# The decoded samples' attention products with queries and probabilities loaded in four 32-column groups and the cache moving

## The chip, the cores and the metric

The kernel runs on one core of a Trainium2 chip. The metric is the device time of one execution in microseconds (us). The time before is the median of three runs, 2102.01 us (2100.24, 2102.01 and 4988.29). One further execution was profiled; every row below is from it.

## The reference

The program is one layer of a hybrid decoder: a prompt of 1024 tokens and eight sequences ("samples") that each decode one token against a carried cache. The change touches only the attention of the samples. Cut to that part:

```python
# samples: kc, vc are the cached 127 keys and values and the new one: (8, 128, 4 kv heads, 64)
kc = concat([cache_k, new_k])[-128:]
vc = concat([cache_v, new_v])[-128:]
s = einsum('qhgd,khd->hgqk', qg, kc) * 64 ** -0.5      # 16 query heads, 4 to a kv head
p = softmax(concat([s, sink]))[..., :-1]
o_b = einsum('hgqk,khd->qhgd', p, vc)                  # then @ w_swa_out
```

So there are 8 samples x 16 heads = 128 score rows of 128 keys, and 128 output rows of 64 channels. Around it stand the projections of all 1032 tokens, the prompt's sliding-window attention, a gated delta rule in chunks with eight heads, an output mix, and a feed-forward part, all in float32.

## The kernel before

The prompt's projections run as three TensorE products of split operands (`mm3`, lines 180 to 182). The prompt's attention is done in four groups of two query tiles (`attention_group`), each group in eight blocks of 128 queries (`attention_block`, called n = 0 to 7). In a block, TensorE makes scores (lines 615 and 616), ScalarE and VectorE mask them into `E` and make a softmax (lines 619 to 638), TensorE transposes `E` into `pt` (line 190), VectorE masks it into `pc` and `pp` (lines 643 and 647), and TensorE multiplies with `V` into `pv` (line 653), which ScalarE copies out (line 655).

The samples' attention is put in at the start of the last group (g = 3). It has three steps. `sample_cache` has loaded keys and values, 128 window positions by 256 channels for each sample, into four tiles named `qst`, and has put the samples' queries into `qa`, a tile whose rows are the 128 channels of two kv heads and which is zero where a head does not use a channel. `sample_keys` transposes the keys in place. `sample_softmax` then makes scores, a softmax over `ps` and `pr` with small sums in `sk`, and the values' product.

Before the change, both products load the cache as the stationary operand, one 128x128 block for each sample and each pair of kv heads, and move eight columns (the queries or probabilities of that sample) past it: sixteen products at line 709 and sixteen at line 736. The scores come out with the keys as rows, so they are copied to `st` (line 710) and transposed. The softmax gives `pr` with one row for each sample and head; `pr` is transposed and copied to `pT` (line 732) for the values. Their product has channels as rows, and sixteen small copies (line 740) put it into `obs`, which goes to memory.

Each engine takes its instructions in one fixed order. A scheduler makes that order when the program is built, from priorities and its own costs; `later(f, by)` gives a step a lower priority. The fillers of group 3 are projections taken in pieces:

```python
if g == 3:
    for _ in range(2 if n < 6 else 18):
        with self.tc.issue_after(self.scored.ins):
            self.later(lambda: next(self.filler), 120)
```

After the attention come the eight delta-rule heads, in which a recursion over eight chunks (lines 946 to 962) alternates TensorE with ScalarE and VectorE while projections fill in between.

Of the kernel before, what the change touches and what calls it, by code (L numbers as in the profile page):

```python
# [18 lines left out]
P = 128  # L19
NP = 1024  # L20
NS = 8
# [43 lines left out]
class Step:  # L65
# [591 lines left out]
    def sample_cache(self, pool, psum, kx, vx):  # L657
        nc, I = self.nc, self.I

        tp = self.t(self.pmf, [NS, 4, P], "mm")  # L660
        for i in range(2):
            self.transpose(tp[:, i, :], kx[:, i, P:136])
            self.transpose(tp[:, 2 + i, :], vx[:, i, :])
        new = self.t(pool, [NS, 512], "new", bufs=1)
        nc.vector.tensor_copy(new, tp.rearrange("b i c -> b (i c)"))
        newd = self.t(self.dr, [1, 2, NS, 256], "newd")
        for c in range(2):
            nc.sync.dma_start(newd[0, c], new[:, c * 256:(c + 1) * 256])

        kv = []  # L670
        for c, (cache, out) in enumerate(((I["cache_swa_k"], self.O[7]), (I["cache_swa_v"], self.O[9]))):
            halves = []
            for b in (0, 4):
                kc = self.t(pool, [P, 4, 256], "qst")
                nc.sync.dma_start(kc, cache[0][b:b + 4].rearrange("b w g d -> w b (g d)"))
                nc.sync.dma_start(kc[0:1], newd[:, c, b:b + 4])
                halves.append(kc)
            kv.append(halves)
            old = lambda a, w: a[0][:, w:w + 127].rearrange("b w g d -> b (w g d)").rearrange("b (s e) -> s b e", s=16)
            with self.tc.issue_after(self.w_load.ins):  # L680
                nc.sync.dma_start(old(out, 0), old(cache, 1))
            nc.sync.dma_start(out[0][:, 127].rearrange("b g d -> b (g d)"), newd[0, c])

        qa = self.t(pool, [P, 2, NS, 8], "qa", bufs=1)
        nc.gpsimd.memset(qa, 0.0)
        for hq in range(16):
            p, r, g = hq // 8, hq % 8, hq // 4
            src = self.qs[(hq % 2) * 64:(hq % 2) * 64 + 64, hq // 2, :]
            nc.vector.tensor_copy(qa[(g % 2) * 64:(g % 2) * 64 + 64, p, :, r], src)
        self.samples = kv, qa  # L690

    def sample_keys(self):
        kc = self.samples[0][0]
        for half in kc:
            for p in range(2):
# [2 lines left out]
                    self.transpose(tp[:, b, :], half[:, b, p * P:(p + 1) * P])  # L698
                self.nc.scalar.copy(half[:, :, p * P:(p + 1) * P], tp)

    def sample_softmax(self, pool, psum):
        nc, I = self.nc, self.I
        (kc, vc), qa = self.samples

        scores = self.t(pool, [P, 2, NS, 8], "st", bufs=1)
        sc = self.t(self.pmf, [P, 2, NS, 8], "mm")
        for b in range(NS):
            for p in range(2):
                nc.tensor.matmul(sc[:, p, b, :], kc[b // 4][:, b % 4, p * P:(p + 1) * P], qa[:, p, b, :], start=True, stop=True)
        nc.vector.tensor_copy(scores, sc)  # L710
        ps = self.t(self.pmf, [P, P], "mm")
        self.transpose(ps, scores.rearrange("k p b r -> k (p b r)"))

        sk = self.t(pool, [P, 8], "sk", bufs=1)
        sinkc = self.t(pool, [P, 1], "sinkc", bufs=1)
        for p in range(2):
            src = I["swa_sinks"][0][p * 8:p * 8 + 8].rearrange("(r o) -> r o", o=1)
            nc.sync.dma_start(sinkc[p * 64:p * 64 + 64, :], src.unsqueeze(0).broadcast_to([NS, 8, 1]))
        nc.vector.tensor_reduce(sk[:, 0:1], ps, axis=AX.X, op=ALU.max)
        nc.vector.tensor_tensor(sk[:, 0:1], sk[:, 0:1], sinkc, op=ALU.max)  # L720
        nc.vector.tensor_tensor(sk[:, 1:2], sinkc, sk[:, 0:1], op=ALU.subtract)
        nc.scalar.activation(sk[:, 2:3], sk[:, 1:2], AF.Exp)
        nc.vector.tensor_scalar_mul(sk[:, 3:4], sk[:, 0:1], -1.0)
        pr = self.t(pool, [P, P], "pr", bufs=1)
        nc.scalar.activation(pr, ps, AF.Exp, bias=sk[:, 3:4], accum_out=sk[:, 4:5])
        nc.vector.tensor_tensor(sk[:, 5:6], sk[:, 4:5], sk[:, 2:3], op=ALU.add)
        nc.vector.reciprocal(sk[:, 6:7], sk[:, 5:6])
        nc.vector.tensor_scalar_mul(pr, pr, sk[:, 6:7])
        ps = self.t(self.pmf, [P, P], "mm")
        self.transpose(ps, pr)  # L730
        pT = self.t(pool, [P, 2, NS, 8], "pT", bufs=1)
        nc.vector.tensor_copy(pT.rearrange("k p b r -> k (p b r)"), ps)
        pv = self.t(self.pmf, [P, 2, NS, 8], "mm")
        for p in range(2):
            for b in range(NS):
                nc.tensor.matmul(pv[:, p, b, :], vc[b // 4][:, b % 4, p * P:(p + 1) * P], pT[:, p, b, :], start=True, stop=True)
        obs = self.t(pool, [P, 8, NS], "obs", bufs=1)
        for hq in range(16):
            p, r, g = hq // 8, hq % 8, hq // 4
            nc.vector.tensor_copy(obs[(hq % 2) * 64:(hq % 2) * 64 + 64, hq // 2, :],  # L740
                                  pv[(g % 2) * 64:(g % 2) * 64 + 64, p, :, r])
        nc.sync.dma_start(self.ob[:, :, NP:NT].rearrange("i p b -> p i b"), obs)
# [1314 lines left out]
```

## Time and profile before

| | value |
|---|---|
| time of the profiled execution | 2099.13 us |
| its span | 2097.4 us |
| granted TensorE clock, mean | 0.983 |
| TensorE (PE) busy | 2027.4 us, 97% |
| weight loads (PEld) busy | 1924.1 us, 92% |
| VectorE (DVE) busy | 1362.2 us, 65% |
| ScalarE (ACT) busy | 902.8 us, 43% |
| share of the chain that ended last: PE / DMA / DVE | 77% / 8% / 6% |

Rows of time read: start in us, duration in us, engine, line, operation, output and inputs, shape, count. A float32 product appears as two records, one for each of its passes, so sixteen products are "x32"; a transpose and a product of split operands have one. Rows by window give, for each engine, busy us and the number of instructions, then the granted TensorE clock (1.00 is full), the share of DMA time and GB/s. PE busy time is modelled and counts an instruction until its result has landed, so it also covers some latency.

### The profile page before, as it was taken

The numbers are of one execution on the slowest core, as the hardware profiler recorded it, in microseconds if no ns is written. First come the engines' busy times: TensorE is split into PE (matmuls) and PEld (weight loads), VectorE is DVE, ScalarE is ACT, GpSimd is POOL, SyncE is SP. The second block draws the span as 40 slices with busy tenths as digits, with TensorE's granted clock in tenths as the row PEclk, the third lists the DMA queues.
The fourth block names the chain that finished last, engine by engine and source line by source line (L and its number), as shares of the span: only waits on it lengthen the run. The fifth ranks groups of instructions, "written<-read, shape, count | busy, mean of one in ns | idle before, by whom it ended". The sixth has DMA issues, their size and how long they took to land.

```text
span 2097.4 us, 41330 instructions
## 1 busy us (share of the span) xinstructions
PE 2027.4 (97%) x16245; PEld 1924.1 (92%) x16245; DVE 1362.2 (65%) x2733; ACT 902.8 (43%) x2233; POOL 520.2 (25%) x594
## 2 busy tenths in 40 slices
PE   7999999999999999989999999999999999999998
PEld 3987778799999999989988999999999999999898
DVE  4756667564736647566554575479876776778875
ACT  3665545433333342442442452245544544544543
POOL 1000000021321211201211000004556556445530
PEclk8999999899999999999999999999999999999999
DMA  7246344152232312312266774413333333487972
GB/s 270 88 140 213 127 148 140 39 147 62 74 83 55 81 58 70 84 36 70 63 193 188 251 230 134 139 58 93 99 97 112 96 97 92 137 295 272 310 233 84
DMA packets 301887, 275.75 MB, mean 131 GB/s; under 512 B 59730, under 2 KB 248111, under 8 KB 301676
## 3 DMA queue, kind: packets, MB, share of 16 engines
q1 hardware_dynamic: 295852, 252.22, 39.2%
q0 software_dynamic: 5552, 20.37, 2.8%
q8 instruction: 127, 2.08, 0.4%
q14 instruction: 68, 0.56, 0.1%
q10 hardware_dynamic: 288, 0.52, 0.1%
HBM read 212.93 MB, written 62.51 MB: 131 GB/s over the span
## 4 chain that ended last, share of the span: by engine, by line
PE 77%; DMA 8%; DVE 6%; ACT 3%; issue 1%; SPq 1%; POOL 1%; DVEq 0%; POOLq 0%; ACTq 0%
PE mm L180 18%; PE mm L181 17%; PE mm L182 17%; PE wv L180 2%; PE wv L182 2%; PE wv L181 2%; PE pv L653 2%; DMA ws<-in_w_ffn_down_dram 1%; PE wy L180 1%; PE wy L182 1%; PE wy L181 1%; DMA raw<-in_w_ffn_down_dram 1%; PE pt L190 1%; PE tp L190 1%; PE sc L615 1%
## 5 line engine op out<-in xcount | busy, mean ns | idle before, releaser
L180 PE MATMUL mm<-b1h,wh 128*128 128x384 f32 (+1 forms) x1520 | 499.0, 330 | 4.9 <-ACT gt L1293 1.8
L181 PE MATMUL mm<-b1l,wh 128*128 128x384 f32 (+1 forms) x1520 | 491.0, 324 | 0.0
L182 PE MATMUL mm<-b1h,wl 128*128 128x384 f32 (+1 forms) x1520 | 490.6, 325 | 0.0
L180 PEld LDWEIGHTS mm<-b1h,wh 128*128 128x128 f32 x1520 | 287.9, 190 | 15.2 <-issue 5.8
L181 PEld LDWEIGHTS mm<-b1l,wh 128*128 128x128 f32 x1520 | 288.0, 190 | 5.4 <-issue 4.3
L182 PEld LDWEIGHTS mm<-b1h,wl 128*128 128x128 f32 x1520 | 287.3, 189 | 3.2 <-issue 2.3
L129 ACT ACTIVATE wh<-raw 128x1024 fp32r<-128x1024 f32 x83 | 87.0, 1048 | 118.5 <-PE mm L181 72.1
L130 DVE TENSOR_TENSOR wl<-raw,wh 128x1024 fp32r<-128x1024 f32 x82 | 101.2, 1235 | 53.6 <-ACT wh L129 52.5
L181 PE MATMUL mm<-pk,w 128*128 128x260 f32 (+1 forms) x440 | 124.9, 284 | 1.1 <-DVE pk L130 1.1
L180 PE MATMUL mm<-pk,w 128*128 128x260 f32 (+1 forms) x440 | 124.8, 284 | 0.0
L182 PE MATMUL mm<-pk,w 128*128 128x260 f32 (+1 forms) x440 | 124.6, 284 | 0.0
L130 DVE TENSOR_TENSOR w<-ws,w 128x512 fp32r<-128x512 f32 x88 | 79.4, 902 | 38.3 <-ACT w L129 38.1
L1625 ACT COPY bml<-mm 128x256 f32<-128x256 f32 (+1 forms) x132 | 48.9, 371 | 100.2 <-PE mm L182 97.1
L180 PE MATMUL mm<-bmh,w 128*128 128x260 f32 (+1 forms) x320 | 90.3, 282 | 0.0
L182 PE MATMUL mm<-bmh,w 128*128 128x260 f32 (+1 forms) x320 | 90.1, 282 | 0.0
L1680 DVE SCALAR_TENSOR_TENSOR fa<-fz,fcw,fa 128x512 f32<-128x512 f32 x88 | 75.0, 873 | 18.3 <-ACT fa L1678 18.0
L180 PE MATMUL mm<-b2h,wh 128*128 128x384 f32 (+1 forms) x256 | 83.3, 328 | 2.5 <-ACT wh L129 2.1
L181 PEld LDWEIGHTS mm<-pk,w 128*128 128x128 f32 x440 | 83.3, 189 | 1.3 <-DVE pk L130 1.3
L181 PE MATMUL mm<-b2l,wh 128*128 128x384 f32 (+1 forms) x256 | 83.6, 327 | 0.4 <-DVE b2l L130 0.4
L180 PEld LDWEIGHTS mm<-pk,w 128*128 128x128 f32 x440 | 83.3, 189 | 0.2 <-ACT bml L1625 0.2
L182 PEld LDWEIGHTS mm<-pk,w 128*128 128x128 f32 x440 | 83.5, 190 | 0.0
L182 PE MATMUL mm<-b2h,wl 128*128 128x384 f32 (+1 forms) x256 | 82.7, 325 | 0.0
(649 smaller groups left out, 5920.6 us busy)
## 6 DMA issues: line engine op xcount, KB each, us to landing
raw<-in_w_in_dram SPq DMA_DIRECT2D x60, 512.0 KB, 4.0
ws<-in_w_ffn_down_dram SPq DMA_DIRECT2D x55, 256.0 KB, 5.4
raw<-xd SPq DMA_DIRECT2D x47, 258.0 KB, 5.3
raw<-in_w_ffn_down_dram SPq DMA_DIRECT2D x47, 256.0 KB, 4.2
raw<-in_w_ffn_gate_dram SPq DMA_DIRECT2D x22, 512.0 KB, 3.8
raw<-in_w_ffn_up_dram SPq DMA_DIRECT2D x22, 512.0 KB
qst<-in_w_mod_dram SPq DMA_DIRECT2D x16, 512.0 KB, 7.8
raw<-in_w_mod_dram SPq DMA_DIRECT2D x16, 512.0 KB, 6.2
```

The source lines that it names most:

```text
L129: self.nc.scalar.activation(hi, x, AF.Copy)
L130: (eng or self.nc.vector).tensor_tensor(lo, x, hi.bitcast(F32), op=ALU.subtract)
L180: mm(ps, whi, xhi, start=first, stop=False, **kw)
L181: mm(ps, whi, xlo, start=False, stop=False, **kw)
L182: self.last_mm = mm(ps, wlo, xhi, start=False, stop=last, **kw).ins
L190: self.nc.tensor.transpose(out, in_, self.ident[:p, :p])
L615: self.scored = nc.tensor.matmul(sc[:, r, 256 - w:256], q, KH[:, lo:lo + w], start=True, stop=False)
L653: nc.tensor.matmul(pv[64 * r:64 * r + 64], V[:, n - back, ch], ps[:, r::2, :], start=back == 0, stop=back == (n > 0))
L1625: self.last_copy = nc.scalar.copy(r[p, i], x[p])
L1680: nc.vector.scalar_tensor_tensor(ai[:, c:e], zi[:, j + c:j + e], col(j), ai[:, c:e], op0=ALU.mult, op1=ALU.add)
```

## The change

The two operands change places in both products. Queries and probabilities are loaded, 32 columns at a time, and the cache moves past them, 128 columns at a time. Sixteen products remain for each of the two; product (i, j) takes loaded columns for sample i of half j % 2 and pair of kv heads j // 2, and writes rows 32j to 32j + 31 of the result, so that four products go to the four 32-column groups of the array, and the four values of i are summed in place. For the sum to be right, `qa` is widened from 128 to 640 columns: eight used columns stand 40 apart, so that each window of 32 has them at another place and zeros elsewhere.

The scores now come out with one row for each sample and head, so the copy to `st` and its transpose are gone. After the softmax, `pr` is transposed as before and copied straight into the same places of `qa` (one copy, in place of the one to `pT`). The values' product has samples and heads as rows, so it is copied (into `pr`) and transposed before the sixteen small copies. The loads of the cache, the transposes of the keys, the softmax and the small copies stay.

```diff
-        qa = self.t(pool, [P, 2, NS, 8], "qa", bufs=1)
+        qa = self.t(pool, [P, 2, 2, 160], "qa", bufs=1)
         nc.gpsimd.memset(qa, 0.0)
+        spread = qa.rearrange("k p h (i c) -> k p h i c", c=40)
...
-            nc.vector.tensor_copy(qa[(g % 2) * 64:(g % 2) * 64 + 64, p, :, r], src)
+            nc.vector.tensor_copy(spread[(g % 2) * 64:(g % 2) * 64 + 64, p, :, :, r], src.rearrange("d (h i) -> d h i", h=2))
...
+    def sample_product(self, out, wide, halves):
+        for i in range(4):
+            for j in range(4):
+                self.nc.tensor.matmul(out[32 * j:32 * j + 32], wide[:, j // 2, j % 2, 32 * i:32 * i + 32],
+                                      halves[j % 2][:, i, j // 2 * P:(j // 2 + 1) * P], start=i == 0, stop=i == 3)
...
-        scores = self.t(pool, [P, 2, NS, 8], "st", bufs=1)
-        sc = self.t(self.pmf, [P, 2, NS, 8], "mm")
-        for b in range(NS):
-            for p in range(2):
-                nc.tensor.matmul(sc[:, p, b, :], kc[b // 4][:, b % 4, p * P:(p + 1) * P], qa[:, p, b, :], start=True, stop=True)
-        nc.vector.tensor_copy(scores, sc)
         ps = self.t(self.pmf, [P, P], "mm")
-        self.transpose(ps, scores.rearrange("k p b r -> k (p b r)"))
+        self.sample_product(ps, qa, kc)
...
-        pT = self.t(pool, [P, 2, NS, 8], "pT", bufs=1)
-        nc.vector.tensor_copy(pT.rearrange("k p b r -> k (p b r)"), ps)
+        nc.vector.tensor_copy(qa.rearrange("k p h (i c) -> k (p h) i c", c=40)[:, :, :, 0:8],
+                              ps.rearrange("k (j i r) -> k j i r", j=4, i=4))
+        ps = self.t(self.pmf, [P, P], "mm")
+        self.sample_product(ps, qa, vc)
+        nc.vector.tensor_copy(pr, ps)
         pv = self.t(self.pmf, [P, 2, NS, 8], "mm")
-        for p in range(2):
-            for b in range(NS):
-                nc.tensor.matmul(pv[:, p, b, :], vc[b // 4][:, b % 4, p * P:(p + 1) * P], pT[:, p, b, :], start=True, stop=True)
+        self.transpose(pv.rearrange("d p b r -> d (p b r)"), pr)
```

The scheduler makes another order of it. TensorE, around the scores' product, before (`mm_3893` are the scores, `mm_3911` their transpose, `E_3966` and `pt_3998` block n = 0; `sc` are the blocks' scores):

```order
L709 MATMUL mm_3893<-qa_3849,qst_3833 128x8 x8
L709 MATMUL mm_3893<-qa_3849,qst_3836 128x8 x8
L615 MATMUL sc_4077<-kh_2708,qst_3333 128x256
L616 MATMUL sc_4077<-kl_2710,qst_3333 128x256
L615 MATMUL sc_4077<-kh_2708,qst_3334 128x256
L616 MATMUL sc_4077<-kl_2710,qst_3334 128x256
L190 MATMUL mm_3911<-ident,st_3892 128x128
L190 MATMUL pt_3998<-ident,E_3966 128x128
L615 MATMUL sc_4084<-kh_2708,qst_3429 128x256
```

The same place with the change (`mm_3892` are the scores; the last of their sixteen products, and what follows):

```order
L705 MATMUL mm_3892<-qst_3833,qa_3849 32x128
L705 MATMUL mm_3892<-qst_3836,qa_3849 32x128
L615 MATMUL sc_4075<-kh_2708,qst_3333 128x256
L616 MATMUL sc_4075<-kl_2710,qst_3333 128x256
L615 MATMUL sc_4075<-kh_2708,qst_3334 128x256
L616 MATMUL sc_4075<-kl_2710,qst_3334 128x256
L615 MATMUL sc_4082<-kh_2708,qst_3429 128x256
L616 MATMUL sc_4082<-kl_2710,qst_3429 128x256
```

The transpose of the scores is gone, and the first transpose of block 0 stands later, behind the transpose of `pr`. After that the two products and the blocks stand as follows, on VectorE, before (`m` and `E` with 4091 and 4076 are block 2, `E_4130` block 3, `pc_4003` block 0, `pc_4060` and `pp_4062` block 1):

```order
L643 TENSOR_TENSOR pc_4003<-pt_3998,triu 128x512
L732 COPY pT_3929<-mm_3927 128x128
L632 TENSOR_TENSOR den_4098<-den_4098,es_4094 128x4
L633 RECIPROCAL den_4098<-den_4098 128x4
L621 COPY_PREDICATED E_4130<-trilu,sc_4131 128x256
L638 TENSOR_SCALAR E_4076<-E_4076,den_4098 128x128
L643 TENSOR_TENSOR pc_4060<-pt_4055,triu 128x512
L647 TENSOR_TENSOR pp_4062<-pt_4055,stril 128x512
L638 TENSOR_SCALAR E_4076<-E_4076,den_4098 128x128
L740 COPY obs_3948<-mm_3931 64x8 x16
```

and with the change (the same blocks have numbers lower by two):

```order
L732 COPY qa_3849<-mm_3923 128x16x8
L624 TENSOR_TENSOR m_4089<-m_4089,sink 128x4
L626 TENSOR_TENSOR es_4092<-sink,m_4089 128x4
L628 TENSOR_SCALAR m_4089<-m_4089 128x4
L643 TENSOR_TENSOR pc_4001<-pt_3996,triu 128x512
L632 TENSOR_TENSOR den_4096<-den_4096,es_4092 128x4
L633 RECIPROCAL den_4096<-den_4096 128x4
L621 COPY_PREDICATED E_4128<-trilu,sc_4129 128x256
L638 TENSOR_SCALAR E_4074<-E_4074,den_4096 128x128 x2
L736 COPY pr_3918<-mm_3926 128x128
L643 TENSOR_TENSOR pc_4058<-pt_4053,triu 128x512
L647 TENSOR_TENSOR pp_4060<-pt_4053,stril 128x512
```

The copy that feeds the values' product stands four instructions earlier, and the copy of the product is new; the sixteen small copies follow two rows further down.

The order of later parts changes too, where nothing was edited. On TensorE this is most in the last two delta-rule heads. One place there, before (`rc` and `o` are the recursion, `tp` the solve of another head, `mm` projections):

```order
L953 MATMUL rc_10730<-s_10728,kd_9893 128x128
L957 MATMUL o_10721<-s_10728,A_9945 128x128
L182 MATMUL mm_10617<-b1h_14_152,wl_10562 128x264
L180 MATMUL mm_10617<-b1h_14_152,wh_10561 128x264
L1037 MATMUL tp_11079<-MR_11076,U_1745_11012 32x32 x19
L946 MATMUL rc_10737<-S_10734,K_8354 128x128
L956 MATMUL o_10721<-S_10734,Q_8355 128x128
L1037 MATMUL tp_11079<-MR_11076,U_1745_11012 32x32 x13
```

and with the change, from the last two of the projection's products that stand ahead of the solve:

```order
L180 MATMUL mm_10615<-b1h_14_152,wh_10559 128x264
L181 MATMUL mm_10615<-b1l_15_153,wh_10559 128x264
L1039 MATMUL tp_11077<-MR_11074,U_1743_11010 32x32 x5
L948 MATMUL rc_10735<-S_10732,K_8352 128x128
L958 MATMUL o_10719<-S_10732,Q_8353 128x128
L1039 MATMUL tp_11077<-MR_11074,U_1743_11010 32x32 x26
L951 MATMUL rc_10738<-y_10734,W_4554 128x128
L1039 MATMUL tp_11077<-MR_11074,U_1743_11010 32x32
```

Thirteen more products of a projection now stand ahead of the solve, and the next recursion step stands within the solve. From here to the end of the heads, 14 of the 27 rows of the recursion (`rc`) stand at another place among their neighbours.

## The prediction

> **What bounds the kernel now.** I read the page first, for the busy shares and the chain that ended last, then the chain around the samples' attention, then windows of that stretch with the granted clock, then its rows in order of time.
>
> ```profile
> PE 2027.4 (97%) x16245; PEld 1924.1 (92%) x16245; DVE 1362.2 (65%) x2733; ACT 902.8 (43%) x2233; POOL 520.2 (25%) x594
> PE 77%; DMA 8%; DVE 6%; ACT 3%; issue 1%; SPq 1%; POOL 1%; DVEq 0%; POOLq 0%; ACTq 0%
> 359.62 4.11 PE mm L709 x32
> 373.25 4.09 PE mm L736 x32
> ```
>
> TensorE is busy for 97% of the span and makes 77% of the chain. Both products of the samples are links of it, with 4.11 and 4.09 us. So time taken from them can reach the end. It does not have to: other engines may be next in that stretch.
>
> ```profile
> 359.30:363.50 4.20, 4.20 (x34) 4.20 (x33) 3.53 (x9) 2.80 (x13) 0.00 (x0) 0.85 0.01 4
> 363.50:372.50 9.00, 7.63 (x30) 6.05 (x29) 5.90 (x27) 6.05 (x28) 0.00 (x0) 0.50 0.14 58
> 372.50:377.30 4.80, 4.80 (x40) 4.69 (x38) 1.80 (x5) 0.96 (x3) 0.00 (x0) 0.86 0.00 0
> 377.30:382.70 5.40, 5.40 (x21) 3.67 (x21) 4.26 (x19) 0.76 (x2) 0.00 (x0) 0.50 0.09 6
> 382.70:388.41 5.71, 3.91 (x26) 2.88 (x26) 2.68 (x10) 3.96 (x15) 0.51 (x1) 1.00 0.10 36
> 359.30:382.70 23.40, 22.03 (x118) 18.61 (x118) 15.49 (x59) 10.57 (x44) 0.00 (x0) 0.64 0.08 25
> 368.12 0.52 PE L181 MATMUL mm<-b1l,wh 128*128 128x384 f32 x1
> 387.49 0.34 PE L181 MATMUL mm<-b1l,wh 128*128 128x384 f32 x1
> ```
>
> The third-last column of a window row is the clock. It falls to 0.50 late in each product and stays there behind it, for 9.0 us after the first and 5.4 us after the second. The same projection then takes 0.52 us, at full clock 0.34. TensorE was not idle in the products; it issued records back to back, but each moved eight columns. The clock drop is thus part of their cost.
>
> **The products.** Removed are two times 32 records of 4.27 us (128x8 moving, bound by the loads of 128 columns). Added are two times 32 records with 32 loaded and 128 moving columns. Line 264 has that shape already, a float32 product into four groups of 32 rows, with 512 moving columns:
>
> ```profile
> 359.46 4.27 PE L709 MATMUL mm<-qa,qst 128*128 128x8 f32 x32
> 180.29 0.62 PE L264 MATMUL mm<-wmh,cTr 128*32 128x512 f32 x2
> 180.31 0.62 PE L264 MATMUL mm<-wml,cTr 128*32 128x512 f32 x2
> 180.75 0.60 PE L264 MATMUL mm<-wmh,cTr 128*32 128x512 f32 x2
> 180.76 0.60 PE L264 MATMUL mm<-wml,cTr 128*32 128x512 f32 x2
> 181.18 1.04 PE L264 MATMUL mm<-raw,cTr 128*32 128x512 f32 x8
> ```
>
> Four records start within 0.02 us of each other, and the next four 0.44 us later: the four groups run side by side, though each has its own loaded and moving operand. A round of 128 columns then takes 0.44 / 4 = 0.11 us; eight rounds (four values of i, two passes) take 0.88 us. Bounds: not below 0.88, and, if the groups did not overlap, 32 x 4.27 / 32 = 4.27 us, no gain. I take the overlap, since the operands stand as at line 264. Entering and leaving a narrower shape costs something:
>
> ```profile
> 406.17 0.33 PE L181 MATMUL mm<-b1l,wh 128*128 128x384 f32 x1
> 406.34 0.34 PE L182 MATMUL mm<-b1h,wl 128*128 128x384 f32 x1
> 406.61 0.65 PE L653 MATMUL pv<-pc,V 128*64 128x256 f32 x4
> 407.09 0.60 PE L653 MATMUL pv<-pp,V 128*64 128x256 f32 x4
> 407.63 0.39 PE L615 MATMUL sc<-kh,qst 128*128 128x256 f32 x1
> ```
>
> The 64-column product starts 0.27 us after a projection whose pitch is 0.17, and the full-width one 0.54 us after a group whose pitch is 0.48: 0.10 and 0.06 us, which I take as 0.1 each way. So a product costs 0.88 + 0.2 = 1.1 us in place of 4.27, and two save 6.3 us of TensorE.
>
> The Trainium skill speaks against narrow shapes here: "TensorEngine Tiling (Array Packing)", Key Properties, says that changing the tiling mode drains TensorE. The rows above agree, and by them the four changes of mode cost 0.4 us in all; without the rule the two products would save 6.7 us.
>
> **The clock.** If the products no longer lower it, the work behind them takes half: 7.63 / 2 = 3.8 us and 5.40 / 2 = 2.7 us, together 6.5 us of TensorE. Bounds: none of it, if something else lowers the clock, and all of it. I take all, since the drops start inside the products and a round of 128 columns for 1 us leaves no such stretch. What else lowers it is a wait:
>
> ```profile
> 249.00:253.00 4.00, 1.38 (x9) 0.77 (x7) 3.05 (x11) 3.90 (x16) 0.00 (x0) 1.00 0.06 17
> 253.00:256.40 3.40, 3.34 (x15) 3.35 (x16) 3.05 (x9) 1.29 (x6) 0.00 (x0) 0.50 0.08 19
> ```
>
> After 4 us with 1.38 us of work the clock was at 0.50 for 3.4 us. The new order makes such a wait possible: TensorE's transpose of `pr` stands early, and must wait for the softmax.
>
> **What the other engines leave of it.** TensorE could give 6.3 + 6.5 = 12.8 us. The blocks of the prompt's attention go on beside it, and their pace has a floor:
>
> ```profile
> 360.64 0.68 DVE L623 TENSOR_REDUCE m<-E 128x4 f32<-128x512 f32 x1
> 368.94 0.69 DVE L623 TENSOR_REDUCE m<-E 128x4 f32<-128x512 f32 x1
> 382.70 0.69 DVE L623 TENSOR_REDUCE m<-E 128x4 f32<-128x512 f32 x1
> 388.41 0.69 DVE L623 TENSOR_REDUCE m<-E 128x4 f32<-128x512 f32 x1
> 394.00 0.68 DVE L623 TENSOR_REDUCE m<-E 128x4 f32<-128x512 f32 x1
> 399.74 0.68 DVE L623 TENSOR_REDUCE m<-E 128x4 f32<-128x512 f32 x1
> 377.37 2.82 DVE L740 COPY obs<-mm 64x8 f32<-64x8 f32 x16 [2.60 <-PE mm L736]
> 365.03 0.29 DVE L719 TENSOR_REDUCE sk<-mm 128x1 f32<-128x128 f32 x1 [0.91 <-PE mm L190]
> ```
>
> Each block reduces its scores once (line 623). At full clock and without the samples the blocks are 5.71, 5.59 and 5.74 us apart, a mean of 5.68, with TensorE waiting. In the disturbed stretch two blocks took 382.70 - 360.64 = 22.06 us. At the clean pace they would take 11.36: at most 10.7 us can be won, not 12.8. VectorE must still do the samples' part: the small copies with 2.82 us, four passes over 128x128 of 0.29 us (reduce, scale, two copies), and six tiny ones that I take at half of that, 0.15: 2.82 + 1.16 + 0.9 = 4.9 us. It does not change with the edit, since one copy goes (`st`) and one comes (of the values' product). VectorE's total of 15.49 us in the stretch of 23.40 would allow 7.9 us. If all of the samples' 4.9 us stands between blocks, 10.7 - 4.9 = 5.8 us are left. I take 6 us, near the lower of these, because the small copies do stand between two blocks in the new order. One transpose goes and one comes on TensorE, so that is nothing.
>
> **The rest.**
>
> ```profile
> L689 DVE COPY qa<-qs x16: 151/170/177, 100.0 to 310.9; 64x8 f32<-64x8 f32 x16
> L685 POOL MEMSET qa<- x1: 204/204/204, 3.7 to 3.7; 128x128 f32 x1
> ```
>
> The wider memset of `qa` is on POOL at 3.7 us (0.2 us, five times the columns at most 1.0 us), and the first copy into it comes at 100 us; that is its cover. The sixteen query copies keep their number and size. SP's queue keeps its DMAs; only the store of `obs` stands one place later, and nothing nearby reads it. Behind the stretch TensorE is busy without a gap, so what is won there is passed on:
>
> ```profile
> 424.00:470.00 46.00, 46.00 (x308) 45.89 (x307) 31.41 (x51) 18.37 (x54) 12.40 (x16) 1.00 0.61 162
> 1040.00:1160.00 120.00, 110.71 (x982) 105.10 (x981) 60.17 (x138) 39.39 (x92) 16.98 (x25) 0.99 0.61 177
> PE rc L953 <- ACT s L951: 4.4, 4, 1.8
> ```
>
> The reordered last heads are the exception. From 1040 to 1160 us TensorE is without work for 9.3 us; in the waits from 960 to 1160 us the recursion's line 953 waited four times for ScalarE, 4.4 us in total. A new order there can give or take a few waits of 1.1 us each. I take nothing for it, with -3 to +11 us as bounds.
>
> **Sum.** 2099.1 - 6.0 = 2093.1 us for the profiled execution. The median of the runs is 2.9 us above that execution, so I predict 2096.0 us, 0.3% below 2102.0.
>
> **Rivals.** (1) Everything that TensorE gives arrives: 2102.0 - 12.8 = 2089.2 us. For it: the chain runs over both products. Against it: the pace of 5.68 us. (2) Nothing arrives: TensorE ends early and waits for the softmax that its next instruction needs, a wait as at 249 us lowers the clock for one or two times 3.4 us, and the blocks keep their times; or the four groups do not overlap. 2102 us. For it: the row of 249 us; against it: two blocks at 22.06 us are far above the pace. By the Trainium skill ("TensorE: Matmul & The Clock Gate", Part 4) a transpose does not count as busy for the clock in the way a product does. That would be a reason for this rival, since transposes are much of what stays in the stretch; the row of 249 us does not tell the two apart, and no run here shows it yet. (3) Slower: the last heads' new order costs more than the samples give. 14 of 27 recursion rows moved; at 1.1 us for each that now waits, ten of them cost 11 us: 2102 - 6 + 11 = 2107 us. It decides from six such waits on. For it: the recursion already waits there. Against it: moved rows may as well wait less, and most still have projections ahead of them. (4) That the change does not do what it says would show as full-width records or a cold clock; it falls under (2).
>
> **How the numbers follow.** Chances: the forecast (a gain of 3 to 9 us) 0.48, rival 1 0.14, rival 2 0.16, rival 3 0.19; 0.03 stay for what no row shows. The range is 2087 to 2108 us: the low end is rival 1 and 2 us of the last heads, the high end rival 3 and 1 us. Every case lies within 2% (42 us), which is about what a measurement of this kernel can tell from no change. So: same 0.97, faster 0.01, slower 0.02.
>
> **What would show it.** In the profile after: the products with 32-column loads, about 1.1 us each, their records starting in fours; the clock at 1.00 through the stretch that is now at 0.50, but for one window at most; blocks 1 to 3 reduced within 16 us, not 22. The forecast is wrong if those blocks still take 20 us or more, if the clock is at 0.50 for over 7 us there, or if the recursion's waits from 960 to 1160 us grow by more than 5 us.

## The result and the profile after

The changed kernel takes 2095.99 us (median of 22 runs, 2089.23 to 2101.16). The kernel before took 2099.64 us beside it (median of 22 runs; one of them took 4988.29 us and is left out of the ratio). The ratio is 0.9983 with a 95% interval of 0.9976 to 0.9991: 3.6 us or 0.17% faster, which is clear of the noise and small. The prediction was 2096.0 us. The number is met, though half by luck: it was taken from a median of 2102.0 for the kernel before, which in more runs is 2099.6, so the gain was forecast at 6.0 us and is 3.6.

The profiled execution has a span of 2097.0 us (2097.4 before). First the page's busy row:

```profile
PE 2020.7 (96%) x16245; PEld 1916.4 (91%) x16245; DVE 1362.4 (65%) x2733; ACT 903.1 (43%) x2233; POOL 516.1 (25%) x594
```

TensorE's rows by time around the two products (start us, duration us, line, operation, shape, count; in brackets idle time before it and what ended it):

```profile
360.65 1.08 PE L705 MATMUL mm<-qst,qa 128*32 128x128 f32 x32
361.66 0.39 PE L615 MATMUL sc<-kh,qst 128*128 128x256 f32 x1
365.33 0.39 PE L615 MATMUL sc<-kh,qst 128*128 128x256 f32 x1 [2.93 <-DVE E L621]
369.18 1.08 PE L705 MATMUL mm<-qst,qa 128*32 128x128 f32 x32 [0.20 <-DVE qa L732]
370.23 0.65 PE L653 MATMUL pv<-pc,V 128*64 128x256 f32 x4
```

The first product holds TensorE for 361.66 - 360.65 = 1.01 us, in place of 4.11 in the chain before; the second holds it for 1.05 us. Behind the first, TensorE now waits 2.93 us, which is new. Windows of the same stretch, before and then after (busy us of PE, PEld, DVE, ACT, POOL with counts, clock, DMA share, GB/s):

```profile
355.00:385.00 30.00, 27.89 (x156) 22.67 (x152) 20.97 (x71) 15.22 (x57) 0.51 (x1) 0.72 0.17 54
```

```profile
355.00:385.00 30.00, 21.10 (x188) 14.91 (x186) 25.06 (x84) 17.81 (x67) 0.51 (x1) 1.00 0.19 61
```

The clock is 1.00 throughout in this profile, where it had a mean of 0.72. TensorE does more instructions in 6.8 us less of busy time, and VectorE is the busiest engine, with 25.06 of 30 us. The blocks' reduces (line 623), with the samples' small copies, after; the last row is that of block 7:

```profile
361.73 0.68 DVE L623 TENSOR_REDUCE m<-E 128x4 f32<-128x512 f32 x1
368.24 0.69 DVE L623 TENSOR_REDUCE m<-E 128x4 f32<-128x512 f32 x1
...
374.03 2.81 DVE L742 COPY obs<-mm 64x8 f32<-64x8 f32 x16
376.87 0.69 DVE L623 TENSOR_REDUCE m<-E 128x4 f32<-128x512 f32 x1
...
403.62 0.69 DVE L623 TENSOR_REDUCE m<-E 128x4 f32<-128x512 f32 x1
```

and block 7 before:

```profile
409.31 0.69 DVE L623 TENSOR_REDUCE m<-E 128x4 f32<-128x512 f32 x1
```

From block 1 to block 7 it took 409.31 - 360.64 = 48.67 us, and now 403.62 - 361.73 = 41.89: the stretch gives 6.8 us. Yet the span is only 0.4 us shorter. To see where the rest went I compare starts of instructions that both programs have: VectorE fills the diagonal of `MR` (line 1002, now 1004) once per delta head. Heads 1, 6, 7 and 8, before and after:

```profile
463.21 0.07 DVE L1002 MEMSET MR<- 128x16 f32 x1
883.33 0.07 DVE L1002 MEMSET MR<- 128x16 f32 x1 [3.79 <-DMA MR<-ud]
964.53 0.07 DVE L1002 MEMSET MR<- 128x16 f32 x1 [2.29 <-DMA MR<-ud]
1047.82 0.07 DVE L1002 MEMSET MR<- 128x16 f32 x1 [3.27 <-DMA MR<-ud]
```

```profile
457.52 0.07 DVE L1004 MEMSET MR<- 128x16 f32 x1
878.14 0.07 DVE L1004 MEMSET MR<- 128x16 f32 x1 [4.05 <-DMA MR<-ud]
961.81 0.07 DVE L1004 MEMSET MR<- 128x16 f32 x1 [2.34 <-DMA MR<-ud]
1048.08 0.07 DVE L1004 MEMSET MR<- 128x16 f32 x1 [3.82 <-DMA MR<-ud]
```

The kernel was 1.1 us behind where the stretch begins (at 355 us; it lost that within the program's first 75 us). It is 5.7 us ahead at head 1, 5.2 at head 6, 2.7 at head 7, and 0.3 behind at head 8. So 5.5 us are given back between 883 and 1048 us. Two more differences follow: some 3.2 us are won between 1122 and 1365 us (same rows compared) and 2.2 lost from there to the end. A second profile of the changed kernel (the first experiment below) has a span of 2093.5 us, 3.9 us shorter than before. The late start and the loss at the end are not in it; the 6.8 us won in the stretch, the loss in the last heads (5.2 us there) and a gain behind 1122 us (2.5 us) are.

### The profile page after: what moved, and what is told of

Same layout as the page of the kernel before. It is cut to its first block, busy times and chain, and to the rows that moved or that the text cites. A ratio compares the mean times of both kernels' runs of the same rounds, so it can differ in the third digit from the quotient of the medians.

```text
span 2097.0 us, 41327 instructions
## 1 busy us (share of the span) xinstructions
PE 2020.7 (96%) x16245; PEld 1916.4 (91%) x16245; DVE 1362.4 (65%) x2733; ACT 903.1 (43%) x2233; POOL 516.1 (25%) x594
## 4 chain that ended last, share of the span: by engine, by line
PE 75%; DMA 8%; DVE 7%; ACT 3%; issue 1%; SPq 1%; POOL 1%; DVEq 0%; POOLq 0%; ACTq 0%
PE mm L180 17%; PE mm L182 17%; PE mm L181 17%; PE wv L180 2%; PE wv L182 2%; PE wv L181 2%; DMA ws<-in_w_ffn_down_dram 1%; PE pv L653 1%; PE wy L180 1%; DMA raw<-in_w_swa_out_dram 1%; PE wy L181 1%; PE wy L182 1%; DMA raw<-in_w_ffn_down_dram 1%; PE mm L264 1%; PE tp L190 1%
## 5 line engine op out<-in xcount | busy, mean ns | idle before, releaser
L129 ACT ACTIVATE wh<-raw 128x1024 fp32r<-128x1024 f32 x83 | 87.0, 1048 | 117.5 <-PE mm L181 71.6
L1627 ACT COPY bml<-mm 128x256 f32<-128x256 f32 (+1 forms) x132 | 49.1, 372 | 96.9 <-PE mm L182 94.4
L182 PE MATMUL mm<-b2h,wl 128*128 128x384 f32 (+1 forms) x256 | 82.9, 326 | 0.0
```

Source lines behind the costliest of these rows:

```text
L129: self.nc.scalar.activation(hi, x, AF.Copy)
L182: self.last_mm = mm(ps, wlo, xhi, start=False, stop=last, **kw).ins
L1627: self.last_copy = nc.scalar.copy(r[p, i], x[p])
```

## The experiments

Two questions were open. **What gives the 6.8 us in the stretch**: the shorter products, or the clock that they no longer lower? **What takes 5.5 us in the last heads**: the new order of their instructions (called theory A in what follows), or something else, such as the places where the clock drops (theory B)? The table has the three intervals in us that the answers rest on, from the starts of line 623 (block 1 to 7) and of the filling of `MR`, and the mean granted clock over the first two. Each interval comes from one profile; times are medians of n runs, to be compared only with the kernel before beside them, and by more than a few us where n is 1. Three of the single runs (2093.28, 2091.88 and 2102.81 us) fall outside what was expected, on both sides; no answer rests on them.

| kernel | block 1 to 7 | clock there | head 6 to 7 | clock there | head 7 to 8 | time (n) | before beside it (n) |
| --- | --- | --- | --- | --- | --- | --- | --- |
| before | 48.67 | 0.82 | 81.20 | 0.96 | 83.29 | 2102.01 (3) | |
| before, again | 48.54 | 0.82 | 81.25 | 0.96 | 82.97 | 2100.13 (1) | 2097.84 (23) |
| after | 41.89 | 1.00 | 83.67 | 0.94 | 86.27 | 2095.99 (22) | 2099.64 (22) |
| after, again | 41.90 | 0.96 | 83.29 | 0.94 | 86.40 | 2095.97 (12) | 2097.84 (23) |
| order as before | 41.68 | 0.92 | 82.27 | 0.94 | 83.67 | 2092.03 (11) | 2097.84 (23) |
| merged copies | 39.38 | 0.96 | 83.13 | 0.94 | 83.78 | 2090.37 (7) | 2097.84 (23) |
| all columns moving | 42.92 | 1.00 | 80.85 | 0.96 | 85.54 | 2093.28 (1) | 2094.70 (1) |
| one group after another | 42.49 | 1.00 | 81.12 | 0.96 | 86.16 | 2091.88 (1) | 2094.70 (1) |
| scores only | 47.45 | 0.82 | 81.14 | 0.96 | 84.76 | 2102.81 (1) | 2094.70 (1) |
| values only | 46.70 | 0.82 | 81.57 | 0.96 | 87.51 | 2097.53 (1) | 2094.70 (1) |
| before, merged copies | 49.09 | 0.83 | 82.11 | 0.94 | 82.88 | 2096.11 (10) | 2100.56 (13) |
| 32 columns moving | 44.33 | 0.92 | 82.61 | 0.94 | 85.71 | 2097.98 (1) | 2100.56 (13) |

**Both kernels again, unchanged.** No edit.

> The kernel before, unchanged, profiled once more, to see how far two executions of one program differ in place. Theory A (the new instruction order of the last delta-rule heads gave back what the samples' stretch won): the same instruction of this execution and of the first profile of before lies within 0.5 us of a constant distance from 330 to 1160 us. Theory B (an execution wins or loses some us in those heads by chance, by where the clock drops): the distance moves by 2 us or more between 860 and 1060 us. Both: the two clock drops at the samples' products are there again, of 10 and 7 us.

> The changed kernel, unchanged, profiled and timed once more beside e3. Both theories: the samples' stretch again gains 6.9 us (block 1 to block 3 in 15.1 us, not 22.1) with the clock at 1.00. Theory A: between 860 and 1060 us the distance to the kernel before shrinks by 5 to 6 us again; ratio 0.998. Theory B: it shrinks by another amount, off by 2 us or more from the first time; ratio 0.997 to 0.999.

Measured: each kernel repeats its own intervals, within 0.4 us in all three columns, and the clock of the stretch before is 0.72 again (355 to 385 us). The changed kernel is at 0.9981 (0.9968 to 0.9995) of the kernel before. So what is won and given back belongs to the programs, not to one execution. One thing differs: in this second profile of the changed kernel the clock falls once behind the wait of TensorE, to 0.50 for some 3.4 us:

```profile
365.40:368.70 3.30, 3.30 (x27) 2.49 (x30) 3.02 (x11) 2.19 (x10) 0.00 (x0) 0.50 0.00 0
```

The stretch takes 41.90 us with it and 41.89 without. One such drop costs nothing there: TensorE has time to spare, with 33.1 of 41.9 us busy. So a drop as such is not what costs in the kernel before; its two are longer, and TensorE is busy in them.

**The new products with the old order.** Half of the sixteen small copies go to ScalarE. That is enough for the scheduler to give the last heads the order of the kernel before, but for single rows (seven of TensorE, three of VectorE) that stand a few places away.

```diff
-            nc.vector.tensor_copy(obs[...], ...)
+            (nc.scalar.copy if hq % 2 else nc.vector.tensor_copy)(obs[...], ...)
```

> The change, with every second of the sixteen small copies of the output on ScalarE. The stretch keeps the change's products; behind it the built order of every engine is that of the kernel before, row for row. Theory A: what the stretch wins (6.9 us, up to 1 us more as VectorE has 1.3 us of copies less) reaches the end: still 6 us or more ahead at 1060 us, ratio 0.9965 to 0.997. Theory B: some of it is lost at other places by chance; ratio 0.998 to 0.999, as for the change.

Measured: 0.9968 (0.9954 to 0.9982), 2092.03 us. The stretch gives 7.0 us, about as in the changed kernel, and head 7 to 8 takes 83.67 us instead of 86.27. At head 8 (1043.99 us) the kernel is 3.8 us ahead, not 6 or more as expected, but block 1 was 1.9 us late: 5.7 of the 7.0 us are kept. Windows of that interval in the kernel before, in the changed one and in this one show what the order does there:

```profile
964.53:1047.82 83.29, 83.05 (x743) 80.94 (x743) 51.89 (x112) 32.08 (x96) 13.69 (x21) 1.00 0.23 61
```

```profile
961.81:1048.08 86.27, 84.51 (x745) 81.47 (x745) 51.20 (x112) 31.96 (x96) 12.67 (x20) 1.00 0.22 59
```

```profile
960.32:1043.99 83.67, 83.67 (x748) 81.60 (x747) 51.80 (x111) 32.13 (x96) 14.63 (x21) 1.00 0.23 60
```

The clock is 1.00 in all three. With the new order TensorE is idle for 1.8 us, not 0.2 or 0.0, and its modelled busy time is 1.5 us above the kernel before. I read the busy part as small products of the recursion that now stand one behind another, each of which counts until its result has landed; no run shows this by itself. The waits in the changed kernel are few and short, the two longest being:

```profile
PE rc L190 <- DVE vn L977: 0.7, 1, 0.7
PE rc L955 <- ACT s L953: 0.5, 1, 0.5
```

Over all kernels the column separates cleanly: 82.9 to 83.8 us in the five profiles with the old order (before twice, this one, and both with merged copies), 84.8 to 87.5 with other orders, and 86.2 to 86.4 in the three with that of the change. The clock is 1.00 there in all with the old order and all with the change's; three of the others (84.76, 85.54 and 85.71 us) had it at 0.98, so part of their time is a drop. Theory A holds for head 7 to 8, with about 3 us. It does not hold for head 6 to 7: there the kernel with one group after another has the changed kernel's order behind the samples and takes 81.12 us, not 83.67, and kernels with the old order stand on both sides. The clock separates them. Windows of the whole interval in the kernel before, in that with one group after another, in the changed one, and in the kernel before with merged copies:

```profile
883.33:964.53 81.20, 74.73 (x672) 70.48 (x671) 50.55 (x110) 29.61 (x92) 12.11 (x19) 0.96 0.21 53
```

```profile
877.82:958.94 81.12, 74.81 (x672) 70.64 (x671) 50.21 (x111) 29.67 (x92) 12.15 (x19) 0.96 0.21 54
```

```profile
878.14:961.81 83.67, 77.04 (x673) 72.32 (x672) 50.48 (x111) 29.66 (x92) 12.09 (x19) 0.94 0.20 51
```

```profile
881.40:963.51 82.11, 76.34 (x671) 72.21 (x670) 50.51 (x110) 29.86 (x92) 12.08 (x19) 0.94 0.21 53
```

In the table, the six profiles with 0.96 take 80.85 to 81.57 us, the six with 0.94 take 82.11 to 83.67, whatever their order and products. The means are 1.7 us apart, which is what one more drop to 0.50 of 3.4 us is worth: half of it. So most of the 2.5 us goes with one more drop of the clock. It is not the order: the kernel before with merged copies has TensorE's order of the kernel before from the first record to the last, and has 0.94. It is not chance from one execution to the next either, since both programs that were profiled twice kept their value. What brings that drop was not tested.

**The small copies merged.** Eight copies of 64x16 in place of sixteen of 64x8, half of them on ScalarE; the old order comes out again.

```diff
-        for hq in range(16):
-            nc.vector.tensor_copy(obs[(hq % 2) * 64:..., hq // 2, :], pv[..., p, :, r])
+        for g in range(4):
+            for s in range(2):
+                r = g % 2 * 4 + s
+                src = pv[..., g // 2, :, r:r + 3:2].rearrange("d b a -> d a b")
+                (nc.scalar.copy if s else nc.vector.tensor_copy)(obs[s * 64:s * 64 + 64, 2 * g:2 * g + 2, :], src)
```

> The change, with the sixteen small copies merged to eight of twice the size, half of them on ScalarE. Behind the stretch the built order is that of the kernel before. Both theories: VectorE's copies fall from 2.8 to 0.7 us and the next blocks come 1 to 2 us sooner than in e3, if these copies stand in the blocks' path, as the prediction took it (8 us won in the stretch); if they do not, as much as e3. Theory A: ratio 0.996 to 0.9965. Theory B: 0.997 to 0.9985.

Measured: 0.9957 (0.9942 to 0.9972), 2090.37 us, the best of all: faster than the kernel before, and 2091.43 us at most where the changed kernel has a median of 2095.97. The stretch takes 39.38 us, 2.5 us less than after. VectorE's row ahead of block 3 shows a part of it:

```profile
371.79 0.16 DVE L744 COPY obs<-mm 64x16 f32<-64x16 f32 x1
371.94 0.69 DVE L623 TENSOR_REDUCE m<-E 128x4 f32<-128x512 f32 x1
```

In the changed kernel 2.81 us of copies end where block 3's reduce starts; here one of 0.16 us does, and the other seven follow behind. Blocks 1 to 3 take 371.94 - 359.50 = 12.44 us, near the 11.36 of the clean pace. The kernel with the old order, in which one copy stands ahead of block 3 too, is as fast so far: 374.93 - 362.50 = 12.43 us. So it is enough that the copies no longer stand ahead of block 3, and the expectation that merging brings it 1 to 2 us sooner fell. The 2.3 us between these two kernels come later. At least 1.4 of them lie from block 6 to 7, which takes 10.98 us there and 9.57 here, right behind a drop of the clock in the kernel with the old order:

```profile
389.60:392.80 3.20, 3.20 (x14) 2.29 (x13) 1.18 (x7) 2.61 (x12) 0.00 (x0) 0.50 0.00 0
```

**All columns moving.** The products of the kernel before, with 128 columns moved past each load instead of eight.

```diff
-  nc.tensor.matmul(sc[:, p, b, :], kc[...], qa[:, p, b, :], start=True, stop=True)
+  nc.tensor.matmul(sc.rearrange("k p b r -> k (p b r)"), kc[...],
+                   qa.rearrange("k p b r -> k (p b r)"), start=b + p == 0, stop=b + p == NS)
```

> The kernel before, with one thing changed in both products of the samples: each of the 64 records moves all 128 columns (all 128 rows of queries or probabilities) instead of eight, and the 32 records of a product are added into one 128x128 result. It loads the same 128x128 operands in the same order, but what it computes for the samples is a sum over them and not each sample's own scores or values: that part of the reference is left out. TensorE issues the same number of records back to back. Clock theory (the clock falls because the records of eight columns keep the array little used while it is never idle): with 128 columns moving the clock stays at 1.00 behind both products, the windows that stood at 0.50 for 9.0 and 5.4 us are gone, each product still takes 4.2 to 4.6 us because its loads bound it, and the blocks 1 to 3 come 3 to 5 us earlier, at most 19 us apart in place of 22.06. Rival (the clock falls for another reason in the stretch, such as the wait for the softmax or the transposes there): the clock is at 0.50 for over 10 us again and the blocks stay at 21 to 23 us. In all 2096 to 2100 us by the first, 2098 to 2103 by the second.

The stretch as a window, and TensorE's rows:

```profile
355.00:385.00 30.00, 24.61 (x179) 20.15 (x178) 23.69 (x81) 17.87 (x71) 0.51 (x1) 1.00 0.18 59
```

```profile
358.04 3.73 PE L709 MATMUL mm<-qa,qst 128*128 128x128 f32 x32
368.73 3.74 PE L736 MATMUL mm<-pT,qst 128*128 128x128 f32 x32
```

The clock theory holds. Sixteen times the columns cost nothing: a product takes 3.73 us, even less than the 4.27 before, whose clock fell inside it. The clock stays at 1.00, and the stretch takes 42.92 us. So 5.75 of the 6.8 us come with products still 3.5 times as long as the new ones. Not all of that is the clock: the scheduler moved some rows of the blocks here too. From block 3 to 4, where the clock is 1.00 in all these kernels, this one takes 381.09 - 377.02 = 4.07 us, and the kernel before and the changed one take 5.71. I put these 1.6 us down to the moved rows; some 4.1 us, three fifths of the 6.8, are left for the clock. That is an estimate, since rows ahead of block 3 moved as well. By the Trainium skill, "TensorE: Matmul & The Clock Gate", Part 1, the clock follows how busy TensorE was in a window of about 3.4 us. The drop of 3.4 us above fits that length. As I read the two rows of this case, they fit only if busy means columns that move and not loads: the records of eight columns filled the same time back to back and lowered it.

**One group after another.** The loops over i and j of the new product are swapped, so that consecutive records go to the same 32 columns of the array.

```diff
-        for i in range(4):
-            for j in range(4):
+        for j in range(4):
+            for i in range(4):
```

> The changed kernel with the two loops of the product swapped: the four records of one group of 32 output rows come one behind another, then those of the next group, so that consecutive records no longer go to four different groups. The same 16 products, operands and results. Overlap theory (what makes a product take 1.0 us is that four groups run side by side): without neighbours in other groups the 32 records take 32 times 0.107 us = 3.4 us a product, with 32 of 128 rows of the array in use at a time; the blocks 1 to 3 come 2 to 5 us later than in the changed kernel (17 to 20 us apart), and if a quarter of the array is too little to keep the clock, a window at 0.50 comes back. Rival (a record is simply short because it loads 32 columns, or the groups overlap whatever their order): 1.0 to 1.3 us a product and blocks at 15 to 15.5 us. In all 2098 to 2101 us by the first, 2096 by the second.

```profile
360.21 2.46 PE L705 MATMUL mm<-qst,qa 128*32 128x128 f32 x32
368.91 2.46 PE L705 MATMUL mm<-qst,qa 128*32 128x128 f32 x32 [0.18 <-DVE qa L732]
```

Neither number was right: 2.46 us, between the 3.4 of the overlap theory and the 1.0 to 1.3 of its rival. The starts of the single records in the trace show why. In the changed kernel they come in fours, 0.02 us within a four and 0.11 us from four to four. Here the first four and the last four of a product come one by one, 0.11 us apart, and those between come in pairs, two in 0.11 us. So a record in one group takes the 0.11 us that the overlap theory had, but TensorE still runs two records at a time for most of the product, which I read as two neighbouring groups. The groups do overlap (2.46 against 1.08 is a factor of 2.3). The Trainium skill, "TensorE: Matmul & The Clock Gate", "Back-to-back issue gap", gives about 81 ns for a record in a stream of loads and products with 128 moving columns. The mean here, 2.46 / 32 = 0.077 us, lies near that, but as a mean over single records and pairs it does not confirm it. The clock stays at 1.00, but 2.46 us is shorter than one drop, so this does not tell what a longer run on a quarter of the array would do. The longer products, 2 x 1.4 = 2.8 us in all, cost the stretch 0.6 us (42.49 against 41.89): their length hardly matters.

**One product alone.** In each, the other product keeps its old form.

Against the kernel before, scores only and then values only (layouts follow):

```diff
-                nc.tensor.matmul(sc[:, p, b, :], kc[...], qa[:, p, b, :], start=True, stop=True)
+        self.sample_product(ps, qa, kc)
```

```diff
-                nc.tensor.matmul(pv[:, p, b, :], vc[...], pT[:, p, b, :], start=True, stop=True)
+        self.sample_product(ps, qa, vc)
```

> Only the scores' product has the new form; the values' product is that of the kernel before, with its 32 records of eight moving columns. If each product brings its own share: the first product takes 1.0 us, the clock stays at 1.00 behind it, and the drop behind the values' product stays (about 5 to 7 us at 0.50). Blocks 1 to 3 then lie 17 to 19 us apart, between 15.14 (both) and 22.06 (none): 3.2 us of product and up to 4.5 us of cold clock are saved, less what VectorE holds back. If the pace of VectorE alone sets the blocks: 15 to 16 us already with this half. If the clock's drop has to do with the softmax's wait, it is there behind the first product too. In all 2095 to 2100 us.

> Only the values' product has the new form; the scores' product is that of the kernel before. If each product brings its own share: the drop behind the scores' product stays (about 9 to 10 us at 0.50), none comes behind the values' product, and blocks 1 to 3 lie 17.5 to 20 us apart. The two halves' gains add up to that of the whole (6.9 us) or more, more if VectorE's pace caps the whole. If one product alone makes the gain, one of the two halves shows 22 us and the other 15. In all 2096 to 2101 us.

With scores only, TensorE's rows and the window behind them:

```profile
365.79 0.39 PE L615 MATMUL sc<-kh,qst 128*128 128x256 f32 x1 [2.93 <-DVE E L621]
367.50 0.41 PE L190 MATMUL mm<-ident,pr 128*128 128x128 f32 x1
369.74 6.89 PE L737 MATMUL mm<-pr,qst 128*128 128x8 f32 x32
```

```profile
368.00:380.00 12.00, 12.00 (x54) 10.97 (x54) 6.68 (x31) 4.33 (x17) 0.00 (x0) 0.50 0.00 0
```

With values only, TensorE's rows and VectorE's sixteen copies:

```profile
373.21 1.08 PE L705 MATMUL mm<-qst,qa 128*32 128x128 f32 x32
378.85 2.81 DVE L749 COPY obs<-mm 64x8 f32<-64x8 f32 x16
382.38 0.41 PE L615 MATMUL sc<-kh,qst 128*128 128x256 f32 x1 [2.73 <-DVE E L621]
```

```profile
363.00:372.00 9.00, 7.63 (x31) 6.69 (x32) 5.36 (x24) 6.24 (x30) 0.00 (x0) 0.50 0.14 58
382.00:388.00 6.00, 5.31 (x26) 4.37 (x26) 3.76 (x11) 1.46 (x4) 0.00 (x0) 0.72 0.10 10
```

The halves give 1.2 and 2.0 us (47.45 and 46.70 against 48.67), together less than half of 6.8. The table tells why: the mean clock over the stretch is 0.82 in both, as in the kernel before, so neither half saves any of the cold time (the time at 0.50). Over all kernels the stretch goes with that column: 46.7 to 49.1 us in the five profiles with 0.82 or 0.83, 39.4 to 44.3 in the seven with 0.92 or more. With scores only the new wait of 2.93 us comes first, the clock falls soon after it (the transpose takes 0.41 us, 0.27 at full clock), and the eight-column product, now 6.89 us, does not bring it back for 12 us. The wait alone does not decide: the changed kernel has it too, and its clock fell in one profile of two. With values only the drop behind the scores is that of the kernel before. Block 3 then comes early all the same (375.90 - 360.66 = 15.24 us behind block 1, where 17.5 to 20 was expected), but VectorE's sixteen copies stand behind it and make TensorE wait 2.73 us until 382.38, and the clock falls there once more. So the expectation that each product brings its own share fell: the cold time moves instead of going, and only without both old products is the gain there. What one drop costs was not separated further.

**The copies merged in the kernel before.** The same edit of the copies as above, without the new products.

> The kernel before, its products unchanged, with the sixteen small copies of the samples' result merged to eight of 64x16 and shared between VectorE and ScalarE, as in the fastest variant so far; the order of every engine stays that of the kernel before, except for the copies themselves. If the copies stand in the path of the blocks only once TensorE's cold stretches are gone (copies need the new products): nothing is won here, the ninth block comes 47 to 49 us after the one at 360 us (48.67 before), and the time is within 1 us of the kernel before. If the copies stand in the path anyway: 1.5 to 2.8 us less in the stretch, and 1.5 to 4 us less in all. In the last heads from 960 to 1060 us nothing is lost, since the order is the old one, by the theory that the order costs 3 to 4.6 us there.

Measured: 49.09 us in the stretch, nothing won. The copies stand in the path only once TensorE's cold stretches are gone. Head 7 to 8 has the old order and takes 82.88 us, as theory A wants. The time is not within 1 us, though: 0.9985 (0.9970 to 0.9999). In the profile this kernel is 2.1 us ahead already at 60 us and wins another 3.2 us between 1122 and 1365 us, neither of them near the edit. Its TensorE order is that of the kernel before from the first record to the last, so that later win is not one of order.

**32 columns moving.** A point between 8 and 128; each record moves the columns of four samples.

```diff
-  nc.tensor.matmul(sc[:, p, b, :], kc[...], qa[:, p, b, :], start=True, stop=True)
+  nc.tensor.matmul(sc[:, p, b - b % 4:b - b % 4 + 4, :], kc[...], qa[:, p, b - b % 4:b - b % 4 + 4, :], start=True, stop=True)
```

> The kernel before, with each of the 64 records moving 32 columns instead of eight (those of four samples; each record overwrites those of the sample before, so the samples' scores and values are left out). The same loads, the same number of records. It is a point between 8 columns, where the clock fell to 0.50 behind both products, and 128 columns, where it stayed at 1.00. If the clock follows the share of time in which columns move, 32 columns in a record that is bound by its load of 0.107 to 0.13 us lie on either side: a clock at 0.50 behind a product, for 3 to 9 us, means that 32 are too few and the ninth block comes 46 to 49 us after the one at 360 us; a clock at 1.00 means that 32 are enough and it comes 42 to 43.5 us after it, as with 128 columns (42.88). I hold the cold clock for the likelier, 0.6.

```profile
357.22 3.65 PE L709 MATMUL mm<-qa,qst 128*128 128x32 f32 x32
369.43 3.66 PE L736 MATMUL mm<-pT,qst 128*128 128x32 f32 x32
```

```profile
362.00:368.00 6.00, 4.47 (x18) 4.40 (x19) 4.55 (x21) 4.13 (x20) 0.00 (x0) 0.50 0.11 44
370.00:396.00 26.00, 22.32 (x155) 17.51 (x155) 16.58 (x60) 13.37 (x55) 1.03 (x2) 1.00 0.12 38
```

This lies in between: a drop of some 6 us behind the first product, none behind the second, and 44.33 us for the stretch. Up to block 3 TensorE and VectorE keep the order of the kernel before here, and blocks 1 to 3 take 377.65 - 358.40 = 19.25 us in place of 22.06. So 10 us less of cold clock give 2.8 us with no change of order; behind block 3 rows moved as with all columns (4.06 us to block 4). One profile cannot say whether 32 columns are at the edge, or whether the first drop has another cause.

## Why the prediction came out right, point by point

- **The products.** 1.1 us each were predicted, 1.01 and 1.05 measured. They replace 4.11 and 4.09 us by the chain, so 6.1 us of TensorE are saved, not 6.3. The overlap read from line 264 was right: the records start in fours, 0.11 us apart. The bound without overlap, 4.27 us, was not reached by swapping the loops (2.46 us), since two records still ran at a time.
- **The clock.** It stayed at 1.00 as predicted, and in the second profile of the changed kernel one drop came, which "one window at most" allowed. The drops did start in the products. But the prediction put the two sources side by side, 6.3 us of shorter products and 6.5 of clock. The runs give the clock some 4.1 of the 6.8 us, by the estimate above, and leave 2.7 for the shorter products with their new order, which were not separated. Length by itself counts little: 2.8 us more of product cost 0.6. Nor has every cold microsecond the price that the prediction gave it: a single drop of 3.4 us cost nothing in the stretch (41.90 us).
- **What the other engines leave.** The cap by the blocks' pace was the step that mattered, and it held: 6.0 us taken, 6.8 measured, of 12.8 that TensorE could give. Blocks 1 to 3 came within 376.87 - 361.73 = 15.14 us, not 22.06 (16 predicted). That the small copies stand between two blocks was right: with all but one behind block 3, blocks 1 to 3 take 12.4 us, and the stretch with merged copies is another 2.5 us shorter. In the kernel before, merging them won nothing there.
- **Rival 2's wait** is there, 2.93 us, and can lower the clock, as with scores only. In the changed kernel it did so in one profile of two, for 3.4 us, at no cost to the blocks. Nothing here tells how transposes count for the clock.
- **The last heads.** This is the term that was mis-sized. I took nothing, within -3 to +11 us; they give back 5.5 us, of which 3 go with the order and most of the rest with one more drop of the clock, which the prediction did not think of there. So "what is won there is passed on" failed. That the gain is 3.6 us and not 6.8 - 5.5 = 1.3 is luck: 2.5 to 3.2 us are won between 1122 and 1365 us, which nobody forecast. The sign I named for the loss was the wrong one too. The recursion's longest wait, on ScalarE, went down from 4.4 to 3.5 us from 960 to 1160 us, and its waits of all kinds together went from 6.7 to 7.3 us, far from 5 more:

```profile
PE rc L955 <- ACT s L953: 3.5, 3, 1.8
```

Rival 3's mechanism is real with 3 of its 11 us, and did not reach the point from which it decides.
- **The base.** The median before was 2102.0 us in three runs and 2099.6 in 22. That moved the number by 2.4 us and made up for the last heads.

Left open: why all kernels other than the one before, the one with merged copies included, win 1.1 to 5.1 us between 1122 and 1365 us, though nothing there was edited and that one keeps its order; and what brings the further drop of the clock in head 6 to 7.

## What to carry to other kernels

Count a product that moves few columns past full loads at the price of the clock behind it, not of its own length: here most of the gain was there with products 3.5 times as long, as long as the clock stayed up, and moving more columns at the same number of loads was free. Before a saving on one engine is added up, read the pace of the loop beside it, and look what next stands between its steps (here sixteen small copies; taken from between the steps and merged, worth another 2.5 us). Where a scheduler orders the program, a local edit reorders steps far away: compare the order there, and try a neutral edit that brings the old order back (here 2092.03 us in place of 2095.97, though the two intervals overlap). Where two profiles differ at a place that nobody edited, take the clock over the whole stretch between two rows that both have, not over a fixed window of time.

## What the runs showed of the hardware that was not expected

- Sixteen times as many moving columns (128 against 8) made a product of 32 records shorter, 3.73 us instead of 4.27; the clock no longer fell inside it.
- Once the clock was at 0.50, 32 records of eight columns, issued back to back for 6.89 us, did not raise it.
- A drop of 3.4 us to 0.50 cost nothing where TensorE waits for VectorE anyway (41.90 us against 41.89), and about half its length, 1.7 us, over head 6 to 7, where it is busy for over 90% of the time.
- Records with 32-column loads and 128 moving columns start four at a time over four groups, every 0.11 us (32 records in 1.08 us), and one or two at a time, every 0.11 us, when eight in a row go to one group (32 records in 2.46 us).
